# Retention's values and gate as products of halves, beside the merge gates, at the end of the attention

## The chip, the cores and the metric

The kernel runs on one core of a Trainium2 chip. The time is the device time of one launch in microseconds (us), the median of several executions. The core has five engines that run beside each other: TensorE (PE, matrix products), VectorE (DVE), ScalarE (ACT), GpSimd (POOL) and SyncE (SP, which here issues DMAs). [...]

## The reference

Two layers work on 512 tokens of width 1024, in float32. Cut to what matters:

```python
h = rmsnorm(x, norm_w) * (1 + scale) + shift
qa, ka, va, za, qr, kr, vr, zr, ga, gr = split(h @ w_in)
y_att = softmax-weighted sum of 3 groups of dilated window attention(qa, ka, va) * silu(za)
y_ret = groupnorm(retention(rotary(qr), rotary(kr), vr)) * gn_w * silu(zr)   # 4 heads of width 256
merged = sigmoid(ga) * (y_att @ w_proj_attn) + sigmoid(gr) * (y_ret @ w_proj_ret)
x = x + gate * (merged @ w_out)
```

`vr`, `zr`, `ga` and `gr` are each a product of `h` (512x1024) with 1024 columns of `w_in`.

## The kernel before, in words

**Numbers as two halves.** Each float32 operand of a product is split into a high and a low part (`split`: ACT copies the high part, DVE subtracts it, which gives the low part), and each product is three matmuls: high by high, high by low, low by high (`mm3`, L180 to L187). Weights come in tiles of 128x1024 (tag `wst`) by DMA on SP's queue and are split into `wh` and `wl`.

**Projections.** `proj_T` (L313) gives 256 columns transposed: 48 matmuls of 128x512. `proj_tok` (L331) gives 256 columns with tokens on the partitions: 96 matmuls of 128x256. `pair` (L719) gives 1024 columns by a scheme of seven products of halves in place of eight (Strassen's kind): both operands are cut in two by two, sums and differences of the parts are formed, and seven products "11", "12", "S1", "S4", "S2", "S3", "22", of 24 matmuls of 128x512 each, 168 in all, are added up to the four quarters of the result. The sums of the weights' parts are formed by DMAs that accumulate into a `wst` tile (issued by POOL); the sums of `h` are formed once by `combine_h` on POOL; those of the retention's result by `combine_y` on DVE.

**A layer in the order of the program** (`layer`, L960). Queries, keys, values and scores of the attention, for two pairs of heads; `softmax(1)` (L517: 16 exponentials on ACT, short vector work on DVE and POOL, then the probabilities are scaled in place, L563 to L569). Then, in turn, `ret_q(0)`, `attend(1, 0)`, `ret_k(0)`, `attend(1, 1)`, `ret_z(0)`. An `attend` (L573) transposes the probabilities on PE (L587), splits them (tag `pt`, four tiles), multiplies them with the values into two PSUM banks (tag `po`, a pool of two) for two rounds, and evicts with ACT (L606) and DVE (L607, L620). Then come four retention heads: `ret_q`, `ret_k` (`proj_T` and a rotation on DVE and POOL), `ret_z` (`proj_T` and a silu), `ret_scores`, `ret_v` (`proj_tok`), and for the head before `ret_out` (group norm) and `ret_y` (transposes on PE, then on DVE the norm's weight and the gate z in one step, L709). Behind them stand `combine_h`, `za`, the gates GA and GR as two `pair`s, `combine_y`, and the merges, among them `merge_ret`, a `pair` that multiplies the retention's result with its weights, and the output, a `pair` again.

**What sets the order.** [...] A scheduler lays each engine's instructions out once, near to the order of the program, and mixes neighbouring steps where one waits for another engine; tile pools (`wst` 7, `wh` and `wl` 4, `pt` 4, `qk` 6, `s` 4, `v` 6, `tmp` 4) hold a step back until a tile is free. So `attend(1, 0)` and `attend(1, 1)` stand on PE within the matmuls of the steps around them.

Of the kernel before, what the change touches and what calls it, by code (L numbers as in the profile page):

```python
# [28 lines left out]
QR, KR, VR, ZR = 5120, 6144, 7168, 8192  # L29
GA, GR = 9216, 10240  # L30
CW = 256
# [30 lines left out]
def trunk(ctx, tc, x, c, positions, norm_w, w_ada, b_ada, w_in, ret_gn_w, w_proj_attn, w_proj_ret,  # L62
          w_out, final_norm_w, c_small, c_decay, out):
    nc = tc.nc
# [9 lines left out]
    def T(tag, dt=F32, shape=(P, S)):  # L74
        n_of[tag] = n_of.get(tag, 0) + 1
        return big.tile(list(shape), dt, tag=tag, name=f"{tag}{n_of[tag]}", bufs=NB[tag])
# [5 lines left out]
    def PS(tag="mm"):  # L82
        n_of[tag] = n_of.get(tag, 0) + 1
        return psp.tile([P, S], F32, tag=tag, name=f"ps_{tag}{n_of[tag]}", bufs=NPS[tag])

    def small(shape, name, bufs=2, dt=F32):
        n_of[name] = n_of.get(name, 0) + 1
        return st.tile(list(shape), dt, tag=name, name=f"{name}{n_of[name]}", bufs=bufs)

    def f(ap):  # L90
        return ap.bitcast(F32)

    def blk(ap, b):
        return ap[:, b * P:(b + 1) * P]
# [7 lines left out]
    xs = [T("s", F32, (P, D)) for b in range(4)]  # L102
    dram = ctx.enter_context(tc.tile_pool(name="dram", bufs=1, space=bass.MemoryType.DRAM))
    x1d = dram.tile([S, D], F32, name="x1d")
    cs = const.tile([P, NSMALL], F32, name="cs")
    rows = T("tmp")[0:64, 0:P]

# [32 lines left out]
    def vec(l, what, k, n=1):  # L140
        i = {"norm": 8 * l, "gn": 16 + 8 * l, "bshift": 32 + 16 * l, "bscale": 40 + 16 * l}[what] + k
        return vecT[:, i:i + n]


    def rsqrt(src, scale, n, name):

        t = small([P, n], name + "_t", 4)
        nc.vector.tensor_scalar(t, src, scale, EPS, op0=ALU.mult, op1=ALU.add)
        r = small([P, n], name, 4)
        nc.gpsimd.tensor_tensor(r, t, mhalf[:, 0:n], op=ALU.pow)  # L150
        return r

    def split(src, hi, lo, in_order=False):

        for ins in (nc.scalar.copy(hi, src), nc.vector.tensor_tensor(lo, src, f(hi), op=ALU.subtract)):  # L155
            if in_order:
                tc.keep_in_program_order(ins)
# [22 lines left out]
    def mm3(ps_ap, pairs, first=True, last=True, skip=False):  # L180

        n, i = 3 * len(pairs), 0
        for (ah, al), (bh, bl) in pairs:
            for a, b_ in ((ah, bh), (ah, bl), (al, bh)):
                nc.tensor.matmul(ps_ap, a, b_, start=first and i == 0, stop=last and i == n - 1,  # L185
                                 skip_group_check=skip)
                i += 1  # L187
# [116 lines left out]
    class Layer:  # L304
# [345 lines left out]
        def ret_k(self, hd):  # L650
            self.rk = self.rotated(KR, hd)

        def ret_z(self, hd):
            t = T("s", F32, (P, 2, S))
            self.rz = [self.silu(ps, t[:, i]) for i, ps in enumerate(self.proj_T(ZR + hd * CW))]

        def ret_v(self, hd):
            self.rv = self.proj_tok(VR + hd * CW, blk)

        def ret_scores(self, hd):  # L660
            dec = T("dec")
# [13 lines left out]
        def ret_out(self, hd):  # L675
            self.rn = []
            for b2 in range(2):
                ps, n_ = PS("aux"), T("tmp")
                for i in range(2):
                    b = 2 * b2 + i  # L680
                    mm3(ps[:, i * CW:(i + 1) * CW],
                        [((blk(self.pts[j][0], b - j), blk(self.pts[j][1], b - j)), self.rv[j])
                         for j in range(b + 1)])
                mv = small([P, 2, 2], "mv")
                for i in range(2):
                    stats = small([P, 6], "stats", 4)
                    nc.vector.bn_stats(stats, ps[:, i * CW:(i + 1) * CW])
                    nc.vector.bn_aggr(mv[:, i], stats)
                rs = rsqrt(mv[:, :, 1], 1.0, 2, "rs")
                for i in range(2):  # L690
                    o = slice(i * CW, (i + 1) * CW)
                    nc.vector.tensor_scalar(n_[:, o], ps[:, o], mv[:, i, 0:1], rs[:, i:i + 1],
                                            op0=ALU.subtract, op1=ALU.mult)
                    self.rn.append(n_[:, o])
            self.rzs = self.rz

        def ret_y(self, hd):
            yt = T("y", F32, (P, 2, S))
            self.ytiles.append(yt)
            ys = [yt[:, 0], yt[:, 1]]  # L700
            for b2 in range(2):
                ps = PS("aux")
                for j in range(2):
                    for i in range(2):
                        nc.tensor.transpose(ps[:, (2 * i + j) * P:(2 * i + j + 1) * P],
                                            self.rn[2 * b2 + j][:, i * P:(i + 1) * P], ident)
                o = slice(b2 * CW, (b2 + 1) * CW)
                for i in range(2):
                    nc.vector.scalar_tensor_tensor(ys[i][:, o], ps[:, i * CW:(i + 1) * CW],  # L709
                                                   vec(self.l, "gn", 2 * hd + i), self.rzs[i][:, o],  # L710
                                                   op0=ALU.mult, op1=ALU.mult)
            self.y += ys


# [157 lines left out]
        def combine_h(self):  # L872
            def terms(r, c, i):
                return [f(ts[2 * c + i][:, :, r * CW:(r + 1) * CW]) for ts in self.parts]
            self.A = self.combined(terms, 4, ["qk", "qk", "s", "s", "qk", "qk", "qk", "qk"], nc.gpsimd, own=False)
            for name, k0, b0 in (("11", 0, 0), ("12", 4, 0), ("22", 4, 2)):
                self.A[name] = lambda k, u, k0=k0, b0=b0: (blk(self.hh[k0 + k], b0 + u), blk(self.hl[k0 + k], b0 + u))


        def gates(self, off, tag):  # L880

            g = [T(tag, F32, (P, 2, S)) for _ in range(4)]
            at = lambda r, c, u: g[2 * r + u][:, c]
            self.pair(self.win, 0, KT, off, self.A, at,
                      lambda r, c, u, ap: nc.scalar.activation(at(r, c, u), ap, AF.Sigmoid))
            return g

        def combine_y(self):

# [70 lines left out]
    def layer(L, xin, on_block):  # L960

        if L.l:
            L.values0(0)
            L.q(0, 0)
            L.k(0, 0)
        for pr in range(2):
            if pr:
                L.q(1, 0)
                L.attend(0, 0)
                L.k(1, 0)  # L970
                L.attend(0, 1)
            for g in (1, 2):
                L.q(pr, g)
                L.scores(pr, g - 1)
                L.k(pr, g)
            if pr:
                L.values0(1)
                L.scores(1, 2)
                L.softmax(1)
            else:  # L980
                L.values(1)
                L.scores(0, 2)
                L.softmax(0)
                L.values(2)
        L.ret_q(0)
        L.attend(1, 0)
        L.ret_k(0)
        L.attend(1, 1)
        L.ret_z(0)
        L.ret_scores(0)  # L990
        L.ret_v(0)
        for hd in range(1, RETH):
            L.ret_q(hd)
            L.ret_out(hd - 1)
            L.ret_k(hd)
            L.ret_y(hd - 1)
            L.ret_z(hd)
            L.ret_scores(hd)
            L.ret_v(hd)
        L.combine_h()  # L1000
        L.za(0)
        L.ret_out(RETH - 1)
        L.za(1)
        L.ga = L.gates(GA, "v")
        L.ret_y(RETH - 1)
        L.gr = L.gates(GR, "pt")
        L.combine_y()
        L.merge_ret()
        L.merge_att()
        L.combine_m()  # L1010
        L.result(xin, on_block)
# [13 lines left out]
    def next_layer(b, x_, r):  # L1025
# [5 lines left out]
        if b == 3:  # L1031
            L1[0].transposed(xn[0:2], 0, 4, KT)
            L1[0].transposed(xn[2:4], 2, 0, KT)

    layer(L0, x, next_layer)
    for m in range(4):
        background.append(gate_row(1, m))
    fw = []

    def result(b, xt, r):  # L1040
# [4 lines left out]
        for i in range(2):  # L1045
# [6 lines left out]
            nc.sync.dma_start(out[b * P:(b + 1) * P, i * S:(i + 1) * S], o)  # L1052

    layer(L1[0], x1d, result)


# [21 lines left out]
```

## Time and profile before

| | us |
|---|---|
| median of 3 runs | 1374.93 (1373.93 to 1375.13) |
| profiled execution | 1373.44 |
| its span | 1371.6 |
| PE busy | 1321.6 (96%) |
| DVE busy | 950.7 (69%) |
| ACT busy | 582.7 (42%) |
| POOL busy | 292.3 (21%) |
| DMA queue of hardware, of software, share of 16 engines | 33.5%, 14.5% |
| mean granted clock of TensorE | 0.994 of full speed |

The span runs from the first instruction to the last; 1.84 us of the profiled execution lie outside of it. PE is busy nearly always, so a stretch's length is the sum of PE's work in it, and time is won where PE has less to do and lost where PE waits. In a row of a timeline, the start of the next row, less the start of this one, is what an instruction really takes, since matmuls are pipelined and overlap in the records.

### The profile page before, as it was taken

Reading aid. Unit: us, or ns where it says so; the run is one execution under the profiler, and the core shown is the slowest. Engines: PE = TensorE matmul, PEld = TensorE weight load, DVE = VectorE, ACT = ScalarE, POOL = GpSimd, SP = SyncE. Lnnn points to the kernel's source line nnn. Section 1 sums busy time; section 2 is a strip of 40 time slices with the busy share of each in tenths; the row PEclk is TensorE's granted clock in tenths of the full one; section 3 lists DMA queues with packets and bytes.
Section 4 is the critical chain, followed back from the end, with each engine's and each line's share of the span. In section 5 each row is a group of like instructions: output and inputs, shape, how many; then the busy total and the mean of one; then the engine's idle time right before and its main releaser. Section 6 shows DMA issues by size and latency. Waiting matters only on the chain.

```text
span 1371.6 us, 18119 instructions
## 1 busy us (share of the span) xinstructions
PE 1321.6 (96%) x6857; PEld 1144.2 (83%) x6857; DVE 950.7 (69%) x1592; ACT 582.7 (42%) x991; POOL 292.3 (21%) x288
## 2 busy tenths in 40 slices
PE   4999999999999999999989999999999999999996
PEld 4779988989889887888768899888989889778875
DVE  5997669586564577766888646656765566868678
ACT  5442433263223245763643325334422323566355
POOL 1200200041121383220230002002121027622124
PEclk9999999999999999999999999999999999999998
DMA  9954245332232228994974323232223232688673
GB/s 315 316 187 128 87 129 184 93 93 70 70 93 86 77 62 184 200 198 140 199 230 154 101 92 92 62 92 77 62 86 100 70 93 68 118 193 201 173 160 101
DMA packets 136647, 179.54 MB, mean 131 GB/s; under 512 B 5936, under 2 KB 97264, under 8 KB 136560
## 3 DMA queue, kind: packets, MB, share of 16 engines
q1 hardware_dynamic: 119152, 144.83, 33.5%
q0 software_dynamic: 17408, 33.56, 14.5%
q8 instruction: 54, 0.88, 0.3%
q14 instruction: 33, 0.27, 0.1%
HBM read 174.17 MB, written 4.19 MB: 130 GB/s over the span
## 4 chain that ended last, share of the span: by engine, by line
PE 79%; DVE 9%; DMA 4%; issue 3%; POOL 2%; ACT 2%; POOLq 0%; SPq 0%; ACTq 0%; DVEq 0%
PE ps_mm L185 67%; PE ps_aux L185 5%; DMA wst<-in_w_in 3%; DVE wl L155 3%; PE ps_po L185 2%; PE ps_po L191 1%; DVE qk L155 1%; PE ps_aux L587 1%; POOL tmp L852 1%; PE ps_aux L191 1%; ACT wh L155 1%; PE ps_po L192 1%; DMA pt<-in_x 1%; PE ps_aux L930 0%; DVE tmp L952 0%
## 5 line engine op out<-in xcount | busy, mean ns | idle before, releaser
L185 PE MATMUL ps_mm<-h,wh 128*128 128x512 f32 x1664 | 524.1, 394 | 5.8 <-POOL h L302 2.1
L155 DVE TENSOR_TENSOR wl<-wst,wh 128x1024 fp32r<-128x1024 f32 (+1 forms) x266 | 344.5, 1300 | 173.4 <-ACT wh L155 167.8
L155 ACT CAST wh<-wst 128x1024 fp32r<-128x1024 f32 (+1 forms) x266 | 277.0, 1045 | 336.1 <-PE ps_mm L185 249.2
L185 PEld LDWEIGHTS ps_mm<-h,wh 128*128 128x128 f32 x1664 | 310.2, 189 | 69.2 <-POOL h L302 2.7
L185 PE MATMUL ps_mm<-h,wl 128*128 128x512 f32 x832 | 325.7, 392 | 0.0
L185 PE MATMUL ps_mm<-wh,h 128*128 128x256 f32 (+1 forms) x1248 | 309.8, 335 | 10.7 <-POOL h L302 2.2
L185 PEld LDWEIGHTS ps_mm<-wh,h 128*128 128x128 f32 x1248 | 236.1, 216 | 27.8 <-ACT h L155 3.3
L185 PE MATMUL ps_mm<-wl,h 128*128 128x256 f32 (+1 forms) x624 | 207.0, 333 | 0.0
L185 PEld LDWEIGHTS ps_mm<-h,wl 128*128 128x128 f32 x832 | 156.8, 189 | 31.8
L185 PEld LDWEIGHTS ps_mm<-wl,h 128*128 128x128 f32 x624 | 134.7, 216 | 5.6
L641 POOL TENSOR_TENSOR tmp<-tmp,tmp 128x512 f32<-128x512 f32 x32 | 50.8, 1598 | 353.2 <-ACT wh L155 259.5
L185 PE MATMUL ps_mm<-wh,qk 128*128 128x512 f32 x384 | 122.4, 394 | 2.6 <-DVE s L806 2.3
L185 PEld LDWEIGHTS ps_mm<-wh,qk 128*128 128x128 f32 x384 | 72.8, 190 | 19.5 <-DVE s L806 2.7
L185 PE MATMUL ps_mm<-wl,qk 128*128 128x512 f32 x192 | 74.5, 393 | 0.0
L185 PE MATMUL ps_mm<-wh,s 128*128 128x512 f32 x224 | 72.1, 391 | 0.0
L155 ACT CAST qk<-ps_mm 128x512 fp32r<-128x512 f32 x48 | 27.7, 584 | 91.2 <-PE ps_mm L185 91.2
L155 ACT CAST qk<-tmp 128x512 fp32r<-128x512 f32 x60 | 36.4, 620 | 69.8 <-POOL tmp L641 49.7
L155 DVE TENSOR_TENSOR v<-ps_mm,v 128x256 fp32r<-128x256 f32 (+1 forms) x52 | 23.9, 460 | 53.9 <-ACT v L155 53.8
L213 DVE SCALAR_TENSOR_TENSOR tmp<-pt,sc,tmp 128x256 f32<-128x256 f32 x126 | 58.1, 494 | 0.3
L155 DVE TENSOR_TENSOR qk<-tmp,qk 128x512 fp32r<-128x512 f32 x60 | 46.9, 798 | 12.6 <-ACT qk L155 12.3
L736 POOL DMA_DIRECT2D wst<-in_w_in x32 | 39.0, 1232 | 76.3 <-DVE wl L155 68.8
L541 POOL COPY mlc<-ml 32x4 f32<-32x4 f32 x32 | 7.1, 221 | 200.3 <-ACT s L532 198.9
(226 smaller groups left out, 1728.0 us busy)
## 6 DMA issues: line engine op xcount, KB each, us to landing
wst<-in_w_in SPq DMA_DIRECT2D x162, 512.0 KB, 3.6
pt<-in_w_ada SPq DMA_DIRECT2D x36, 512.0 KB, 5.1
wst<-in_w_in POOLq DMA_DIRECT2D x32, 512.0 KB, 7.4
wst<-in_w_proj_ret POOLq DMA_DIRECT2D x16, 512.0 KB, 6.1
wst<-in_w_out POOLq DMA_DIRECT2D x16, 512.0 KB, 5.9
wst<-in_w_proj_ret SPq DMA_DIRECT2D x12, 512.0 KB, 5.3
wst<-in_w_out SPq DMA_DIRECT2D x12, 512.0 KB, 4.1
wst<-in_w_proj_attn SPq DMA_DIRECT2D x8, 512.0 KB, 4.4
```

Of the source, the lines that this page charges most:

```text
L155: for ins in (nc.scalar.copy(hi, src), nc.vector.tensor_tensor(lo, src, f(hi), op=ALU.subtract)):
L185: nc.tensor.matmul(ps_ap, a, b_, start=first and i == 0, stop=last and i == n - 1, skip_group_check=skip)
L191: nc.tensor.matmul(ps_ap, st[0], mv, start=first, stop=False, skip_group_check=skip)
L192: nc.tensor.matmul(ps_ap[:, 0:P], st[1], mv[:, 0], start=False, stop=last, skip_group_check=skip)
L213: nc.vector.scalar_tensor_tensor(acc, w_, c_, acc, op0=ALU.mult, op1=ALU.add)
L541: (nc.gpsimd if cc % 2 else nc.vector).tensor_copy(mlc[32 * b:32 * b + 32, cc], ml0[32 * cc:32 * cc + 32, b])
L587: nc.tensor.transpose(blk(ps, j), src, ident)
L641: nc.gpsimd.tensor_tensor(a, a, b_, op=ALU.subtract if i == 0 else ALU.add)
L736: nc.gpsimd.dma_start(t, part(r, c, i), accum_op=ALU.add)
L852: eng.tensor_tensor(t, t, a, op=ALU.subtract)
```

## The change

`vr` and `zr` are now computed by `pair`, for all four heads at once, and so are GA and GR; the four pairs stand in a row behind the attention (`keep`), and their results go, through tiles of tag `v`, to four arrays in DRAM (`kept`). The retention loads a head's raw values and its silu(z) from there (`ret_vz`) and splits the values; the merge loads the gates (`kept_rows`). `combine_h` moves ahead of the four pairs. The multiplication by silu(z) moves into `ret_out`, one DVE instruction a tile, and `ret_y` evicts on ACT with the norm's weight as its scale. `ret_q(0)` and `ret_k(0)`, which stood between the attends, stand behind the four pairs.

```diff
-        def ret_z(self, hd):
-            t = T("s", F32, (P, 2, S))
-            self.rz = [self.silu(ps, t[:, i]) for i, ps in enumerate(self.proj_T(ZR + hd * CW))]
-
-        def ret_v(self, hd):
-            self.rv = self.proj_tok(VR + hd * CW, blk)
+        def ret_vz(self, hd):
+            raw, self.rz = T("s", F32, (P, 4, CW)), T("s", F32, (P, 4, CW))
+            for o, what in ((raw, "vr"), (self.rz, "zr")):
+                nc.sync.dma_start(o, kept[self.l, what][:, hd * CW:(hd + 1) * CW].rearrange("(b p) j -> p b j", p=P))
+            self.rv = []
+            for i2 in range(2):
+                t = T("v", F32R, (P, 2, 2, CW))
+                split(raw[:, 2 * i2:2 * i2 + 2], t[:, :, 0], t[:, :, 1])
+                self.rv += [(t[:, j, 0], t[:, j, 1]) for j in range(2)]
...
-            self.rzs = self.rz
+                nc.vector.tensor_tensor(n_, n_, self.rz[:, 2 * b2:2 * b2 + 2].rearrange("p b j -> p (b j)"), op=ALU.mult)
...
-                    nc.vector.scalar_tensor_tensor(ys[i][:, o], ps[:, i * CW:(i + 1) * CW],
-                                                   vec(self.l, "gn", 2 * hd + i), self.rzs[i][:, o],
-                                                   op0=ALU.mult, op1=ALU.mult)
+                    nc.scalar.activation(ys[i][:, o], ps[:, i * CW:(i + 1) * CW], AF.Copy,
+                                         scale=vec(self.l, "gn", 2 * hd + i))
...
-            self.A = self.combined(terms, 4, ["qk", "qk", "s", "s", "qk", "qk", "qk", "qk"], nc.gpsimd, own=False)
+            self.A = self.combined(terms, 4, ["qk"] * 6 + ["s"] * 2, nc.gpsimd, own=False)
...
+        def keep(self, off, what, act):
+
+            def done(r, c, u, ap):
+                o = T("v")
+                act(o, ap)
+                nc.sync.dma_start(kept[self.l, what][(2 * r + u) * P:(2 * r + u + 1) * P, c * S:(c + 1) * S], o)
+            self.pair(self.win, 0, KT, off, self.A, lambda r, c, u: T("pt"), done)
+
+        def kept_rows(self, what, tag):
+            res = []
+            for b in range(4):
+                t = T(tag, F32, (P, 2, S))
+                nc.sync.dma_start(t, kept[self.l, what][b * P:(b + 1) * P].rearrange("p (c j) -> p c j", c=2))
+                res.append(t)
+            return res
...
-        L.ret_q(0)
         L.attend(1, 0)
-        L.ret_k(0)
         L.attend(1, 1)
-        L.ret_z(0)
+        L.combine_h()
+        L.keep(VR, "vr", nc.scalar.copy)
+        L.keep(ZR, "zr", lambda o, ap: L.silu(ap, o))
+        L.keep(GA, "ga", L.sigmoid)
+        L.keep(GR, "gr", L.sigmoid)
+        L.ret_q(0)
+        L.ret_k(0)
+        L.ret_vz(0)
         L.ret_scores(0)
-        L.ret_v(0)
         for hd in range(1, RETH):
...
-        L.combine_h()
         L.za(0)
         L.ret_out(RETH - 1)
         L.za(1)
-        L.ga = L.gates(GA, "v")
+        L.ga = L.kept_rows("ga", "v")
         L.ret_y(RETH - 1)
-        L.gr = L.gates(GR, "pt")
+        L.gr = L.kept_rows("gr", "pt")
         L.combine_y()
```

The order moves at three places. PE before, at the start of `attend(1, 0)` of the first layer (`ps_mm49` and `ps_mm50` are products of `ret_z(0)`, `ps_aux62` and `ps_aux63` take the attend's first transposes):

```order
L185 MATMUL ps_mm49_2838<-h4_99,wl44_2835 128x512
L185 MATMUL ps_mm50_2863<-h1_96,wh43_2828 128x512
L587 MATMUL ps_aux62_2600<-cs_76,s11_2153 128x128 x4
L587 MATMUL ps_aux63_2608<-cs_76,s12_2398 128x128 x4
L185 MATMUL ps_mm50_2863<-h5_100,wh43_2828 128x512
L185 MATMUL ps_mm50_2863<-h1_96,wl43_2829 128x512
L185 MATMUL ps_mm50_2863<-h1_96,wh43_2828 128x512
L185 MATMUL ps_mm50_2863<-h5_100,wh43_2828 128x512
```

PE of the changed kernel, the same place (`ps_mm48` is the product "S1" of `vr`, with `qk31` and `qk32` from `combine_h`; `ps_po11` and `ps_po12` are the attend's products with the values):

```order
L186 MATMUL ps_mm48_2840<-wl44_2790,qk31_2677 128x512
L186 MATMUL ps_mm48_2840<-wh44_2789,qk32_2678 128x512
L588 MATMUL ps_aux62_2530<-cs_84,s11_2161 128x128 x4
L588 MATMUL ps_aux63_2538<-cs_84,s12_2406 128x128 x4
L588 MATMUL ps_aux64_2546<-cs_84,s9_1946 128x128 x4
L192 MATMUL ps_po11_2562<-pt37_2535,v9_1199 128x256
L193 MATMUL ps_po11_2562<-pt37_2535,v9_1199 128x128
L192 MATMUL ps_po12_2563<-pt37_2535,y5_1255 128x256
L193 MATMUL ps_po12_2563<-pt37_2535,y5_1255 128x128
L588 MATMUL ps_aux65_2554<-cs_84,s9_1946 128x128 x3
```

Of `vr`'s pair two products stand ahead of the attend: the 24 matmuls of "11" in the middle of the last `scores(1, 2)`, the 24 of "S1" behind it. From the first transpose on, nothing but the two attends stands on PE until the last of them. PE before, within the attends (`ps_mm52` is `ret_v(0)`):

```order
L191 MATMUL ps_po14_2655<-pt40_2628,v14_2342 128x256
L192 MATMUL ps_po14_2655<-pt40_2628,v14_2342 128x128
L185 MATMUL ps_mm52_2982<-wh45_2944,h2_97 128x256
L185 MATMUL ps_mm52_2982<-wl45_2945,h2_97 128x256
L185 MATMUL ps_mm52_2982<-wh45_2944,h6_101 128x256
L185 MATMUL ps_mm52_2982<-wh46_2950,h3_98 128x256
L185 MATMUL ps_mm52_2982<-wl46_2951,h3_98 128x256
L587 MATMUL ps_aux68_2768<-cs_76,s10_1959 128x128 x4
L185 MATMUL ps_mm52_2982<-wh46_2950,h7_102 128x256
L587 MATMUL ps_aux69_2776<-cs_76,s10_1959 128x128 x3
```

PE of the changed kernel, at the attends' end (`ps_po19` is the product "12" of `vr`):

```order
L192 MATMUL ps_po18_2658<-pt44_2632,v13_2295 128x256
L193 MATMUL ps_po18_2658<-pt44_2632,v13_2295 128x128
L192 MATMUL ps_po18_2658<-pt43_2625,v14_2350 128x256
L193 MATMUL ps_po18_2658<-pt43_2625,v14_2350 128x128
L192 MATMUL ps_po18_2658<-pt44_2632,v14_2350 128x256
L193 MATMUL ps_po18_2658<-pt44_2632,v14_2350 128x128
L186 MATMUL ps_po19_2793<-wh41_2747,h3_106 128x512
L186 MATMUL ps_po19_2793<-wl41_2748,h3_106 128x512
```

The "12" of `vr` takes a `po` bank as the attends do, and stands behind them all; no matmul of another step is left between. DVE before, `combine_y` among the splits of GA's weights (`wl84` to `wl88`, `v28`, `s20` and `tmp99` are `combine_y`):

```order
L155 TENSOR_TENSOR wl84_4869<-wst76_4733,wh84_4868 128x1024
L155 TENSOR_TENSOR v28_5296<-y13_4220,v27_5295 128x512
L155 TENSOR_TENSOR v28_5296<-y14_5000,v27_5295 128x512
L155 TENSOR_TENSOR s20_5290<-y11_3280,s19_5289 128x512
L155 TENSOR_TENSOR s20_5290<-y12_3750,s19_5289 128x512
L838 TENSOR_TENSOR tmp99_5310<-y12_3750,y14_5000 128x512
L155 TENSOR_TENSOR wl85_4899<-wst79_4822,wh85_4898 128x1024
```

DVE of the changed kernel, `combine_y` (`tmp98`, `tmp99`, `v60`, `h10`, `qk54`) among the splits of `merge_ret`'s own weights (`wl121` to `wl123`):

```order
L842 TENSOR_TENSOR tmp98_5253<-y11_4339,y13_4925 128x512
L156 TENSOR_TENSOR wl121_5386<-wst87_5381,wh121_5385 128x1024
L156 TENSOR_TENSOR v60_5240<-y14_5210,v59_5239 128x512
L842 TENSOR_TENSOR tmp99_5254<-y12_4632,y14_5210 128x512
L156 TENSOR_TENSOR h10_5246<-tmp98_5253,h9_5245 128x512
L156 TENSOR_TENSOR s28_5568<-y10_2561,s27_5567 128x1024
L856 TENSOR_TENSOR tmp98_5253<-tmp98_5253,y11_4339 128x512
L156 TENSOR_TENSOR h10_5246<-tmp99_5254,h9_5245 128x512
L156 TENSOR_TENSOR wl122_5390<-wst88_5382,wh122_5389 128x1024
```

Of the 22 DVE instructions of `combine_y`, 19 now stand among those of `merge_ret`; the gates' 168 and 168 matmuls, under which they stood, are gone from there.

## Rows read from the trace of the kernel before

**Rows 1.** The page's part 1: each engine's busy time and share.
```profile
PE 1321.6 (96%) x6857; PEld 1144.2 (83%) x6857; DVE 950.7 (69%) x1592; ACT 582.7 (42%) x991; POOL 292.3 (21%) x288
```

**Rows 2.** A window of layer 1: length; PE, PEld, DVE, ACT, POOL busy; clock; DMA.
```profile
940.26:960.50 20.24, 20.24 (x91) 16.71 (x91) 16.63 (x42) 11.43 (x39) 10.23 (x15) 1.00 0.25 79
```

**Rows 3.** Timeline of PE, ret_v's and ret_z's matmuls: start, length, engine, line, tiles.
```profile
322.13 0.40 PE L185 MATMUL ps_mm<-wh,h 128*128 128x256 f32 x2
...
322.49 0.40 PE L185 MATMUL ps_mm<-wh,h 128*128 128x256 f32 x2
...
327.20 0.62 PE L185 MATMUL ps_mm<-h,wh 128*128 128x512 f32 x2
...
327.88 0.39 PE L185 MATMUL ps_mm<-h,wh 128*128 128x512 f32 x1
```

**Rows 4.** Timeline of PE in layer 1: last scores, what follows, first transposes.
```profile
940.20 0.22 PE L192 MATMUL ps_aux<-qk,qk 128*128 128x128 f32 x1
940.26 0.45 PE L185 MATMUL ps_mm<-h,wl 128*128 128x512 f32 x1
...
960.51 1.03 PE L587 MATMUL ps_aux<-cs,s 128*128 128x128 f32 x8
961.30 0.48 PE L185 MATMUL ps_mm<-h,wh 128*128 128x512 f32 x1
```

**Rows 5.** Timeline of DVE, softmax of layer 1.
```profile
942.30 1.23 DVE L155 TENSOR_TENSOR wl<-wst,wh 128x1024 fp32r<-128x1024 f32 x1
...
951.83 0.68 DVE L155 TENSOR_TENSOR qk<-tmp,qk 128x512 fp32r<-128x512 f32 x1
...
953.28 1.23 DVE L155 TENSOR_TENSOR wl<-wst,wh 128x1024 fp32r<-128x1024 f32 x1
...
955.89 1.29 DVE L563 TENSOR_TENSOR s<-s,f 128x512 f32<-128x512 f32 x2
```

**Rows 6.** The window of the attends, ps_po's instructions alone.
```profile
294.40:318.80 24.40, 7.32 (x60) 7.24 (x60) 5.43 (x9) 2.38 (x4) 1.00 0.21 66
```

**Rows 7.** Groups of DVE by form, 294.4 to 318.8, the attends of layer 0.
```profile
L155 DVE TENSOR_TENSOR pt<-ps_aux,pt 128x512 fp32r<-128x512 f32 x6 | 3.9, 682 | 0.3 <-ACT pt L155 0.2
L620 DVE TENSOR_TENSOR y<-ps_po,y 128x256 f32<-128x256 f32 x5 | 3.0, 620 | 0.4 <-PE ps_po L192 0.4
L607 DVE TENSOR_TENSOR y<-ps_po,y 128x256 f32<-128x256 f32 x4 | 2.4, 629 | 0.8 <-ACT y L606 0.8
...
L155 DVE TENSOR_TENSOR pt<-ps_aux,pt 128x384 fp32r<-128x384 f32 x2 | 1.1, 543 | 0.0
```

**Rows 8.** Groups of ACT by form, 274 to 318.8.
```profile
L155 ACT CAST pt<-ps_aux 128x512 fp32r<-128x512 f32 x6 | 3.3, 589 | 3.6 <-PE ps_aux L587 3.6
...
L606 ACT COPY y<-ps_po 128x256 f32<-128x256 f32 x4 | 2.4, 654 | 0.6 <-PE ps_po L192 0.6
```

**Rows 9.** Timeline of PE: two places behind idle time, in brackets.
```profile
16.83 1.02 PE L225 MATMUL ps_aux<-one,tmp 128*128 128x1 f32 x4 [10.40 <-DVE tmp L213]
...
25.83 0.63 PE L185 MATMUL ps_mm<-h,wl 128*128 128x512 f32 x1
...
690.79 0.50 PE L185 MATMUL ps_mm<-wh,qk 128*128 128x512 f32 x1 [2.26 <-DVE s L806]
```

**Rows 10.** Windows: behind that second wait; one retention head.
```profile
691.90:695.40 3.50, 3.50 (x10) 2.71 (x9) 3.39 (x11) 1.45 (x4) 0.00 (x0) 0.51 0.99 308
...
1043.70:1096.20 52.50, 52.50 (x304) 46.54 (x304) 30.00 (x53) 15.21 (x22) 7.47 (x6) 1.00 0.29 86
```

**Rows 11.** Groups of DVE by form in that head.
```profile
L155 DVE TENSOR_TENSOR wl<-wst,wh 128x1024 fp32r<-128x1024 f32 x9 | 11.8, 1308 | 13.0 <-ACT wh L155 12.9
```

**Rows 12.** Windows: merge_ret, then GA, of layer 0.
```profile
591.26:623.90 32.64, 32.64 (x146) 27.03 (x144) 23.67 (x25) 17.18 (x20) 7.24 (x6) 1.00 0.92 205
508.63:550.37 41.74, 40.71 (x179) 32.53 (x180) 32.40 (x40) 24.76 (x34) 16.49 (x13) 1.00 0.70 154
```

**Rows 13.** The page's part 6: a weight tile's load, from issue to landing.
```profile
wst<-in_w_in SPq DMA_DIRECT2D x162, 512.0 KB, 3.6
```

More of the change, by code (lines that the diff above doesn't have):

```diff
@@ L104, in trunk @@
     x1d = dram.tile([S, D], F32, name="x1d")
+    kept = {(l, what): dram.tile([S, D], F32, name=f"{what}{l}") for l in range(DEPTH) for what in ("vr", "zr", "ga", "gr")}
     cs = const.tile([P, NSMALL], F32, name="cs")
@@ L874, in terms, with sigmoid @@
                 return [f(ts[2 * c + i][:, :, r * CW:(r + 1) * CW]) for ts in self.parts]
-            self.A = self.combined(terms, 4, ["qk", "qk", "s", "s", "qk", "qk", "qk", "qk"], nc.gpsimd, own=False)
+            self.A = self.combined(terms, 4, ["qk"] * 6 + ["s"] * 2, nc.gpsimd, own=False)
             for name, k0, b0 in (("11", 0, 0), ("12", 4, 0), ("22", 4, 2)):
                 self.A[name] = lambda k, u, k0=k0, b0=b0: (blk(self.hh[k0 + k], b0 + u), blk(self.hl[k0 + k], b0 + u))
[L880 to L886, printed above, removed]
+        def keep(self, off, what, act):
[4 more added lines that the diff above has]
+            self.pair(self.win, 0, KT, off, self.A, lambda r, c, u: T("pt"), done)
+        def sigmoid(self, o, ap):
+            nc.scalar.activation(o, ap, AF.Sigmoid)
+        def kept_rows(self, what, tag):
[5 more added lines that the diff above has]
+            return res
         def combine_y(self):
@@ L984, in layer @@
                 L.values(2)
+        L.attend(1, 0)
+        L.attend(1, 1)
+        L.combine_h()
[3 more added lines that the diff above has]
+        L.keep(GR, "gr", L.sigmoid)
         L.ret_q(0)
-        L.attend(1, 0)
         L.ret_k(0)
-        L.attend(1, 1)
-        L.ret_z(0)
+        L.ret_vz(0)
         L.ret_scores(0)
-        L.ret_v(0)
         for hd in range(1, RETH):
@@ L996, in layer @@
             L.ret_y(hd - 1)
-            L.ret_z(hd)
+            L.ret_vz(hd)
             L.ret_scores(hd)
-            L.ret_v(hd)
-        L.combine_h()
         L.za(0)
```

## The prediction

> **What bounds the kernel now.** I read the busy times first: PE 1321.6 of 1371.6 us, no other engine over 70% [rows 1]. Then the windows by stage: behind the attention's last scores PE is busy for all 20.24 us up to the attends [rows 2], and the retention's windows are the same (one is shown below); no wait is left there that a change could take away. So a stage gets shorter only by fewer or narrower matmuls, and longer by whatever leaves PE without work. The change does both, and I cost the two sides apart. In a row of the timeline the reader is to look at the distance between starts, not at the length.
>
> **What it removes on PE.** The step of a group of three matmuls (high by high, high by low, low by high) is 0.36 us for 128x256, from 322.13 to 322.49, and 0.68 us for 128x512, from 327.20 to 327.88 [rows 3]: 0.120 and 0.227 each. Per layer `ret_v` has 4 x 96 of the first, 46.1 us, and `ret_z` 4 x 48 of the second, 43.5 us; the two pairs that replace them have 2 x 168 of the second, 76.2 us. That saves 13.4 us a layer, 26.9 in both. GA and GR are pairs before and after and cost PE the same.
>
> **What it uncovers: the softmax.** Before the change, `ret_q(0)`, `ret_k(0)` and a part of `ret_z(0)` lie between the last scores and the first transposes, from 940.26 to 960.51 [rows 4]. In the changed order that place holds "S1" of `vr`, 24 matmuls or 5.4 us. The chain under it is scores, maxima, exponentials, denominators, factors, and the scaling of the probabilities: its first two instructions on DVE begin at 955.89 and take about 0.65 each [rows 5], so what the first transposes need is there at 956.6, 16.3 us behind the last scores. 16.3 less 5.4 leaves PE idle for 10.9 us a layer. The low end: the two weight splits of 1.23 and two qk splits of some 0.6 that stand within the chain [rows 5] belong to other steps and could fall out of it, 3.7 us, which leaves 7.2. The high end: as many other splits get in as two more of 1.3, so 13.5. `combine_h`'s work for POOL stands there too, but between softmax's short copies, so I take the middle value, which is what this chain has taken.
>
> **What it uncovers: the attends.** Before, both attends are spread over 24.4 us of PE work, of which their products take 7.32 [rows 6]; eight transposes step in 0.79 [rows 4], so their 30 take 3.0. Now they stand alone. PE needs 10.3 us for them. DVE needs for each three splits of 0.68, one of 0.54, two additions of 0.63 and four of 0.62 [rows 7]: 6.3, for both 12.6, with two splits of `combine_h` of 0.68 between them 13.9. In addition, each step waits for the one before: four transposes (0.4), the copy on ACT (0.59) [rows 8], the split (0.68), the products, then the eviction (0.65 and 0.63) [rows 7, 8] before a bank of the pool of two is free, and for a second attend once more. Walking through the printed order with these durations I come to 18.3 us, an estimate, which is near the middle between the bounds 13.9 (DVE without a gap) and 24.4 (as long as before). The wait is 18.3 less 10.3, 8.0 a layer, from 3.6 to 14.1.
>
> **The clock.** [...] Behind the longer wait of 10.40 us at the start, matmuls of 128x512 still take 0.63 us in place of 0.39, 9.0 us later [rows 3, 9]: a loss of 4.5. [...] I take 3.2.
>
> [...]
>
> **The retention.** A head has 52.50 us of PE and 30.00 of DVE [rows 10]. Without V and Z, PE has 52.5 less 11.5 less 10.9, 30.1. DVE loses the splits of V's and Z's four weight tiles, 4 x 1.31 [rows 11], and is at 24.8; the splits of the loaded values, the multiplication with z and the moved eviction change it by less than 1 us. That is 82% in place of 57%, and there is less foreign work to hide `ret_out`'s norm, the new multiplication and the transposes of `ret_y`, one after the other. I take 1.5 us of waits a layer (0 to 4).
>
> **The merge.** `combine_y` was hidden under GA and GR, 168 matmuls each. Now 19 of its 22 DVE instructions stand in `merge_ret`. That stage has DVE 23.67 of 32.64 us for 146 matmuls [rows 12], so 27.6 for all 168 (38.1 us); 19 instructions of 128x512 at 0.68 [rows 7] add 12.9: 40.5. DVE is then later than PE by 2.4, and as the products ask for the parts in an order, I take 3.0 a layer (0, if much of it is done under `za`, to 5).
>
> **What I cost at nothing.** The four pairs in a row: GA alone lost 41.74 less 40.71, 1.0 us [rows 12], and the weights' splits (1.3 us, two for 24 matmuls or 5.4 us) fit. The results to DRAM are 16 stores a pair's column on SP's queue, of 2 MB for 38 us of PE; a weight tile lands 3.6 us after its issue [rows 13], and `wst` holds seven. The loads back are needed long after the stores, and `ret_vz(0)` comes behind GA and GR, 76 us later. If this cover fails, it is rival D.
>
> **The sum.** 2 x (10.9 + 8.0 + 3.2 + 1.5 + 3.0) = 53.2, less 26.9, gives +26.3. On the profiled execution's 1373.44 that is 1399.7; the median lies 1.5 above it, so 1401. With all low ends 2 x 12.5 less 26.9, 1371.5; with all high ends (13.5, 14.1, 4.5, 4, 5) 2 x 41.1 less 26.9, 1428.7.
>
> **The rivals.**
> B, not slower: the waits take their low ends. The saving of 13.4 us a layer is certain, so the kernel is no slower if softmax and attends together leave PE idle for less than that: 7.2 + 3.6 + 1.7, 12.5, gives 1373 on the median. For it: the chain before was not hurried, since nothing waited for it, and DVE's foreign work in it is half other. Against it: both low ends are needed at once, and the exponentials on ACT and the steps of the attend follow from data.
> C, DVE and its chain bound the retention: the load of z, the norm, the multiplication, the transposes and the eviction leave PE waiting in every head. At 3 us for each of 8 heads in place of my 3.0 in all, +21: 1422. For it, DVE at 82%; against it, ACT at 15.21 of 52.5 [rows 10], which takes the eviction over.
> D, weights come late: a pair's second weight tile stands behind the stores on SP's queue and misses its time by one landing, 3.6 us [rows 13], in the three later pairs of each layer: +21.6, 1423. For it, one queue for both; against it, seven tiles and the mean traffic.
> [...]
>
> **How the numbers follow.** My forecast 0.63, B 0.14, C 0.09, D 0.07, E 0.07. The forecast's own range is 1386 to 1414: each of the two large terms can be off by some 3 us a layer. To leave out no more than 2 in 10, the range takes in E and half of C and D, and the upper half of B: 1375 to 1422. A measurement of this kernel can tell some 0.2%, 2.75 us, from no change. B is half below 1372.2, half within; a little of the forecast's low edge is added: faster 0.08, same 0.07, slower 0.85.
>
> **What would show it.** The saving: retention heads of about 30 us, V's and Z's pairs of 38 each. The softmax: a wait of PE of about 11 us behind "S1", put down to DVE's scaling, in each layer. The attends: a stretch of some 18 us, PE busy for little more than half of it, with waits on DVE's splits and evictions. The clock: a granted clock near 0.5 there, and for some us of the product "12". `merge_ret`: waits on DVE's splits of its weights or of `combine_y`. I am wrong if PE's idle time from the last scores to the product "12" is under 13 us a layer, if waits in the retention or in the four pairs are as large as those in the attends, or if PE's busy time falls by something else than 27 us and the clock's loss.

## The result and the profile after

The changed kernel takes 1435.28 us (median of 4 runs, 1434.16 to 1440.25) against 1374.72 us, a ratio of 1.0459 (95% interval 1.0439 to 1.0479). It is slower by some 60 us; 26 were forecast. The profiled execution took 1435.49 us, 62.05 more than that of before.

First the page's part 1 and two lines of its part 2, 40 slices of the span, in tenths:

```profile
PE 1318.2 (92%) x6377; PEld 1119.1 (78%) x6377; DVE 1013.4 (71%) x1608; ACT 640.6 (45%) x1071; POOL 330.0 (23%) x320
...
PE   4899999859999999989989999994899999998996
...
PEclk9999999979999999999999999997999999999998
```

PE is busy for only 3.4 us less than before [rows 1], though it has 26.9 us less to do at full speed: by that, matmuls at a lower granted clock (a mean of 0.972 over the span) took some 23.5 us back (an estimate; a part of them stands where PE waits for others anyway). Idle time grew by 65.5 us, and the 9th and the 28th slice of 40, one in each layer, show a dip in PE and in the clock. The groups of PE's waits name them (engine, line and what it waited for; us in total, times, longest):

```profile
PE ps_aux L588 <- DVE s L564: 27.5, 2, 14.6
...
PE ps_mm L186 <- ACT h L156: 9.2, 6, 3.4
PE ps_mm L186 <- DVE pt L810: 8.5, 6, 2.1
PE ps_aux L588 <- DVE pt L156: 6.8, 6, 2.2
...
PE ps_mm L186 <- ACT h L783: 4.3, 2, 2.1
...
PE ps_aux L710 <- DVE tmp L700: 3.0, 2, 1.5
```

The first is the transposes' wait for the scaled probabilities, once in each layer; L810 and L783 are the pairs' results, L156 with `pt` the attends' splits, L156 with `h` the sums' splits (3.4 us of it in each `merge_ret`), L700 the multiplication by z of the last head.

PE's timeline in layer 1, which answers to [rows 4]: the last scores end at 968.47, "S1" runs from there, and the first transposes begin 21.2 us later, 14.62 of them idle.

```profile
968.41 0.22 PE L193 MATMUL ps_aux<-qk,qk 128*128 128x128 f32 x1
968.47 0.68 PE L186 MATMUL ps_mm<-wh,qk 128*128 128x512 f32 x2
969.75 0.50 PE L186 MATMUL ps_mm<-wl,qk 128*128 128x512 f32 x1 [0.60 <-DVE wl L156]
...
974.64 0.39 PE L186 MATMUL ps_mm<-wh,qk 128*128 128x512 f32 x1
989.65 1.73 PE L588 MATMUL ps_aux<-cs,s 128*128 128x128 f32 x7 [14.62 <-DVE s L564]
```

What DVE did in that time (against [rows 5]), and POOL beside it:

```profile
969.61 0.74 DVE L508 TENSOR_TENSOR s<-ps_aux,cs 128x256 f32<-128x256 f32 x2
970.28 1.64 DVE L156 TENSOR_TENSOR wl<-wst,wh 128x1024 fp32r<-128x1024 f32 x1
...
972.51 1.12 DVE L156 TENSOR_TENSOR qk<-tmp,qk 128x512 fp32r<-128x512 f32 x1
...
974.14 3.16 DVE L156 TENSOR_TENSOR qk<-tmp,qk 128x512 fp32r<-128x512 f32 x1
977.22 1.22 DVE L525 TENSOR_TENSOR m<-mx,mx 128x8 f32<-128x8 f32 x1
978.36 1.21 DVE L156 TENSOR_TENSOR wl<-wst,wh 128x1024 fp32r<-128x1024 f32 x1
979.50 0.16 DVE L528 TENSOR_SCALAR nm<-m 128x8 f32<-128x8 f32 x1
...
988.79 1.31 DVE L564 TENSOR_TENSOR s<-s,f 128x512 f32<-128x512 f32 x2
```

```profile
967.32 5.75 POOL L860 TENSOR_TENSOR tmp<-tmp,h 128x512 f32<-128x512 f32 x3 [0.63 <-DVE qk L156]
...
974.52 2.22 POOL L847 TENSOR_TENSOR tmp<-h 128x512 f32<-128x512 f32 x1
976.82 1.60 POOL L848 TENSOR_TENSOR tmp<-tmp,tmp 128x512 f32<-128x512 f32 x1
...
987.42 2.12 POOL L559 COPY f<-f0c 32x2 f32<-32x2 f32 x8 [4.72 <-DVE f L556]
```

The maxima (`nm`) are ready 11.0 us behind the last scores (968.47 to 979.50); before the change it was 3.4 (940.26 to 943.64):

```profile
943.64 0.17 DVE L527 TENSOR_SCALAR nm<-m 128x8 f32<-128x8 f32 x1
```

The splits of the weights (`wl`) and of `combine_h`'s sums (`qk`) stand ahead of them, and one split of 0.68 us [rows 5] takes 3.16 while POOL adds. From the maxima to the scaling it is 9.3 us. In layer 0 the whole takes 23.2 us.

Windows (columns as in [rows 2]): both attends of layer 0 and of layer 1; a stretch of 32.5 us of the retention; the last 120 matmuls of `merge_ret`.

```profile
297.69:317.68 19.99, 14.84 (x91) 13.60 (x91) 15.21 (x24) 8.80 (x17) 4.96 (x5) 0.76 0.01 2
989.65:1009.80 20.15, 14.84 (x90) 13.45 (x91) 15.35 (x25) 9.27 (x18) 4.95 (x5) 0.75 0.00 1
```

```profile
508.20:540.70 32.50, 32.50 (x169) 27.85 (x168) 23.88 (x42) 11.60 (x19) 8.44 (x6) 1.00 0.30 90
```

```profile
618.53:653.68 35.15, 29.58 (x121) 23.61 (x121) 33.92 (x42) 19.56 (x28) 8.26 (x7) 0.95 0.71 152
```

The attends alone take 20 us at a mean granted clock of 0.76. The retention has no gap; its stretch holds 168 matmuls where a head has 158, so that ten (2.3 us) are of a neighbouring step, and a head takes 30.2 us, as forecast. And `merge_ret`'s 120 matmuls (27.2 us at full speed) take 35.15, with DVE busy for 33.92 of them, where 146 took 32.64 and DVE 23.67 before [rows 12].

The bill by stages, start to start on PE, per layer (layer 0, layer 1), against before:

| stage | lost, us |
|---|---|
| fewer and wider matmuls | -13.4, -13.4 |
| last scores to first transposes, less 5.4 of "S1" | 17.8, 15.7 |
| the attends, less 10.3 of PE's work | 9.7, 9.8 |
| the four pairs, over 168 x 0.227 each, less what GA and GR lost before | 4.2, 8.5 |
| the retention's loop | 0, 0 |
| `merge_ret` (46.1 in place of 38.1) and the last `ret_y` | 9.9, 9.9 |
| elsewhere | 1.8, 1.8 |

The sum is 30.0 and 32.3 us, 62.3 together, against the 62.1 us by which the span grew.

### The profile page after: what moved, and what is told of

Read it like the earlier page. It is cut to its first block, busy times and chain, and to the rows that moved or that the text cites. A ratio compares the mean times of both kernels' runs of the same rounds, so it can differ in the third digit from the quotient of the medians.

```text
span 1433.7 us, 17686 instructions
## 1 busy us (share of the span) xinstructions
PE 1318.2 (92%) x6377; PEld 1119.1 (78%) x6377; DVE 1013.4 (71%) x1608; ACT 640.6 (45%) x1071; POOL 330.0 (23%) x320
## 5 line engine op out<-in xcount | busy, mean ns | idle before, releaser
L156 DVE TENSOR_TENSOR wl<-wst,wh 128x1024 fp32r<-128x1024 f32 (+1 forms) x290 | 374.2, 1295 | 208.8 <-ACT wh L156 199.1
L186 PE MATMUL ps_mm<-h,wh 128*128 128x512 f32 x1408 | 447.7, 395 | 5.8 <-POOL h L303 2.1
L156 ACT CAST wh<-wst 128x1024 fp32r<-128x1024 f32 (+1 forms) x290 | 302.2, 1045 | 298.5 <-PE ps_mm L186 171.7
L186 PEld LDWEIGHTS ps_mm<-h,wh 128*128 128x128 f32 x1408 | 263.5, 189 | 60.1 <-POOL h L303 2.7
L186 PE MATMUL ps_mm<-wh,h 128*128 128x512 f32 (+1 forms) x864 | 258.9, 379 | 22.4 <-ACT h L156 9.2
L186 PE MATMUL ps_mm<-h,wl 128*128 128x512 f32 x704 | 276.1, 393 | 0.0
L186 PEld LDWEIGHTS ps_mm<-wh,h 128*128 128x128 f32 x864 | 182.1, 229 | 46.5 <-ACT h L156 11.8
L186 PE MATMUL ps_mm<-wh,qk 128*128 128x512 f32 x576 | 180.8, 392 | 8.2 <-ACT h L783 4.3
L186 PE MATMUL ps_mm<-wl,h 128*128 128x512 f32 (+1 forms) x432 | 162.0, 376 | 0.0
L186 PEld LDWEIGHTS ps_mm<-wh,qk 128*128 128x128 f32 x576 | 108.8, 189 | 32.5 <-ACT h L783 5.1
L156 ACT CAST qk<-tmp 128x512 fp32r<-128x512 f32 x60 | 36.9, 620 | 87.9 <-POOL tmp L642 64.9
L156 ACT CAST qk<-ps_mm 128x512 fp32r<-128x512 f32 x48 | 27.7, 584 | 90.3 <-PE ps_mm L186 90.3
L186 PE MATMUL ps_po<-wh,h 128*128 128x512 f32 (+1 forms) x224 | 66.3, 369 | 0.2 <-DVE y L621 0.2
L186 PEld LDWEIGHTS ps_mm<-wl,qk 128*128 128x128 f32 x288 | 54.3, 189 | 15.5 <-DVE wl L156 4.2
L156 DVE TENSOR_TENSOR qk<-tmp,qk 128x512 fp32r<-128x512 f32 x60 | 56.4, 941 | 12.7 <-ACT qk L156 11.9
L186 PEld LDWEIGHTS ps_mm<-wh,s 128*128 128x128 f32 x288 | 54.1, 188 | 13.9 <-ACT pt L804 2.9
```

## The experiments

Each ran beside the kernel before on the same chip, and ratios to that are compared (the changed kernel's is 1.0459). Lines are those of the changed kernel.

**e1: no sums.** The edit:

```diff
-            self.A = self.combined(terms, 4, ["qk"] * 6 + ["s"] * 2, nc.gpsimd, own=False)
-            for name, k0, b0 in (("11", 0, 0), ("12", 4, 0), ("22", 4, 2)):
+            self.A = {}
+            for name, k0, b0 in (("11", 0, 0), ("12", 4, 0), ("22", 4, 2), ("S1", 0, 2), ("S4", 4, 2), ("S2", 0, 2), ("S3", 0, 0)):
```

> The sums of h's halves (combine_h: GpSimd additions, ScalarE and VectorE splits) are left out; the products take unsummed parts of h in their place, as many matmuls as before. Theory A (combine_h's work gets into the softmax's chain, on VectorE's queue and by slowing VectorE while GpSimd adds): from the last scores to the first transposes it takes about 15 us in place of 21.2 to 23.2, and the kernel about 1421 us (2 x 7 less than 1435). Rival (the chain is longer because of the pair's weight splits and because ScalarE starts late): the chain stays above 19 us, the kernel above 1429 us.

Measured: 1419.22 us, ratio 1.0328 (1.0304 to 1.0352). PE from its last product to the transposes, and DVE's maxima:

```profile
278.33 0.39 PE L186 MATMUL ps_mm<-wh,h 128*128 128x512 f32 x1
288.09 1.94 PE L588 MATMUL ps_aux<-cs,s 128*128 128x128 f32 x8 [9.38 <-DVE s L564]
```

```profile
276.52 0.17 DVE L525 TENSOR_TENSOR m<-mx,mx 128x8 f32<-128x8 f32 x1
276.72 0.17 DVE L528 TENSOR_SCALAR nm<-m 128x8 f32<-128x8 f32 x1
...
287.25 1.29 DVE L564 TENSOR_TENSOR s<-s,f 128x512 f32<-128x512 f32 x2
```

The last scores end at 273.02, so the chain takes 15.1 us and not 23.2, and the maxima are there after 3.7. Theory A holds: `combine_h`'s work is what lengthened the chain. Of the 7.3 us by which the maxima are later in the changed kernel (layer 1), some 4.4 are longer instructions there: splits of 3.16 and 1.12 us in place of 0.68, one of 1.64 in place of 1.21, and L525 of 1.22 in place of 0.17 (an estimate from the rows); the rest is more instructions ahead of the maxima, `combine_h`'s two splits among them. `merge_ret` stays at 46.1 in layer 0 (48.3 in layer 1).

**e2: the sums late.** `combine_h`'s results go to `["s"] * 4 + ["y"] * 4` in place of `["qk"] * 6 + ["s"] * 2`.

> combine_h's results go to tiles that the attention still holds (4 of s, 4 of y), so its splits cannot start before the attends; S1 then stands among the attends' matmuls and not ahead of them. Theory A: the chain shrinks to about 15 us, its 5.4 us of cover by S1 is lost but comes back as cover in the attends: about 1422 us. Rival A2 (GpSimd's additions alone, which need only tmp tiles, slow VectorE): the chain stays at 19 us or more, all of it idle, and the kernel is at 1432 us or above. Rival (weight splits): as A2, but VectorE's splits have their usual length of 0.7 and 1.2 us in the chain.

Measured: 1424.22 us, ratio 1.0364 (1.0339 to 1.0390). The chain takes 13.8 us, 13.60 of them idle, and GpSimd does none of its additions there, since they wait behind the splits.

```profile
274.27 0.22 PE L193 MATMUL ps_aux<-qk,qk 128*128 128x128 f32 x1
288.09 1.30 PE L588 MATMUL ps_aux<-cs,s 128*128 128x128 f32 x5 [13.60 <-DVE s L564]
```

Theory A again; A2 was not tested by it, as the additions moved too.

**e3: cover at the attends.** e2's tiles and

```diff
+        L.ret_q(0)
         L.attend(1, 0)
+        L.ret_k(0)
         L.attend(1, 1)
...
-        L.ret_q(0)
-        L.ret_k(0)
         L.ret_vz(0)
```

> ret_q(0) and ret_k(0) stand between the attends again, with combine_h's results in s and y tiles as in e2; everything else as in the changed kernel. Theory (the loss at softmax and attends is missing cover): 14.6 us of ret_q(0) and ret_k(0) and 5.4 us of the product 11 cover a chain of 15 to 16 us, and the attends have 24 + 18 matmuls as cover; per layer some 15 + 5 us of waits and 3 us of slow clock go: about 1390 us. Rival (VectorE is the limit there, the wait only moves into the attends and the pairs): less than 20 us gained, above 1415 us.

Measured: 1405.29 us, ratio 1.0224 (1.0208 to 1.0241), between the two. The wait for the softmax is gone (the transposes follow the product "11" at once), but a wait of 8.2 us stands within the attends, for splits of `pt`.

**e5 and e6: the sums on VectorE.** In the changed kernel (e5) and in e3 (e6): `nc.vector` in place of `nc.gpsimd` in `combine_h`.

> The changed kernel with one edit: combine_h adds on VectorE in place of GpSimd. Theory A2 (what stretches VectorE's splits in the softmax's chain, 3.16 us for one of 0.68, is GpSimd adding from SBUF beside it): splits in the chain have 0.7 and 1.2 us again; VectorE has 6 additions of 0.68 of its own there (4 us), so the chain shrinks from 21.2 to 23.2 to about 18 to 19 us: some 1428 us. Rival (VectorE is simply overloaded there): 22 additions of 0.68 more on it make the chain and the attends longer, 1436 us or above.

> The kernel of e3 with combine_h's additions on VectorE. In e3 two weight splits took 4.26 us together and others 3.5 to 3.9 beside GpSimd's additions, and the attends waited 8.2 + 1.5 + 2.2 us. Theory A2: these waits fall to some 5 us a layer in all: about 1391 us (1405 less 2 x 7). Rival (VectorE has too much work in the attends, whoever slows it): 1403 us or above.

Measured: e5 1436.12 us, ratio 1.0459 (1.0437 to 1.0480), no gain; e6 1395.85 us, ratio 1.0170 (1.0139 to 1.0202), by the ratios some 7 us better than e3. In e5 every split in the chain has its usual length again (0.68 and 1.21), and the chain takes 20.3 us, but VectorE's own additions stand in it, and the attends take 22.6 us in place of 20.0. So the stretching goes where GpSimd's additions go, but the load on VectorE decides there, in whichever form it comes. In e6 GpSimd still has the scaling and the rotation to do, and two weight splits of 1.23 us took 4.26 together beside it. The same two took 4.26 in e3, and the wait for the splits of `pt` stays (8.3 us in e6, 8.2 in e3): `combine_h`'s additions on GpSimd did not cause that wait, and where e6 gains was not traced.

```profile
284.83 1.23 DVE L156 TENSOR_TENSOR wl<-wst,wh 128x1024 fp32r<-128x1024 f32 x1
...
292.27 4.26 DVE L156 TENSOR_TENSOR wl<-wst,wh 128x1024 fp32r<-128x1024 f32 x2
```

```profile
291.76 1.49 POOL L570 TENSOR_TENSOR s<-s,f 128x512 f32<-128x512 f32 x1
293.21 4.45 POOL L642 TENSOR_TENSOR tmp<-tmp,tmp 128x512 f32<-128x512 f32 x2
```

**e4 and e7 to e12: cover for `combine_y`.** GA and GR go back to their place ahead of the merges, which needs a second `combine_h` there, since its eight tiles cannot be kept through the retention:

```diff
-        L.keep(GA, "ga", L.sigmoid)
-        L.keep(GR, "gr", L.sigmoid)
...
+        L.combine_h(["qk", "qk", "s", "s", "qk", "qk", "qk", "qk"])
         L.za(0)
         L.ret_out(RETH - 1)
         L.za(1)
-        L.ga = L.kept_rows("ga", "v")
+        L.ga = L.gates(GA, "v")
         L.ret_y(RETH - 1)
-        L.gr = L.kept_rows("gr", "pt")
+        L.gr = L.gates(GR, "pt")
```

> GA and GR are computed at their old place ahead of the merges, with a second combine_h there; V and Z as in the changed kernel. Theory B (merge_ret lost the cover of combine_y, 9.9 us a layer): merge_ret is back at 38 to 39 us, and 2 x 9 us come back: about 1417 us. Rival (merge_ret waits for weights, since 3 loads and 4 accumulations stand close together): merge_ret stays above 44 us, the kernel above 1430 us. Rival (the second combine_h slows VectorE in the last heads): merge_ret recovers, but heads get longer by 3 us or more: about 1424 us.

e4 took 1462.47 us, ratio 1.0645 (1.0626 to 1.0664). `merge_ret` is back at 38.1 us in both layers, but GA waits once for 23.5 us in each:

```profile
PE ps_mm L186 <- DVE tmp L626: 46.9, 2, 23.5
```

GA's matmuls need the PSUM banks of za, which its silu (L625 on ACT, L626 on DVE) frees; the silu needs `tmp` tiles, and the second `combine_h` holds them through 38 us of additions on GpSimd, from 520 to 558 us in layer 0; the silu begins at 557. Six kernels tried to get that work out of the way: e7 (za ahead of it, and `v` in place of `s` tiles), e8 (as e7, with e6's start and za(0) between the attends), e9 (e6 with the second `combine_h` on VectorE, ahead of za), e10 (as e9, za(0) between the attends), e11 (as e10, the second `combine_h` behind ret_out(3) and za(1)), e12 (as e10, 6 `tmp` and 6 `wst` tiles).

> As e4 (GA and GR at their old place, a second combine_h on GpSimd), but za's two multiplications stand ahead of the second combine_h on GpSimd and its results need no s tile, which e4 waited for. Theory B (combine_y lost its cover): no wait of 23 us; merge_ret at 38 to 39 us; about 1436 - 2 x 9 = 1418 us. Rival (merge_ret waits for its weights): merge_ret stays above 44 us. Rival (GA and GR beside combine_h and combine_y lose as much as merge_ret gains): 1430 us or above, with waits of 5 us and more in GA.

> V and Z as pairs, with cover for all three places: ret_q(0), ret_k(0) and za(0) between the attends, combine_h's additions on VectorE with results in s and y tiles, GA and GR ahead of the merges as in the kernel before. Theory (the loss was only missing cover): of the saved 26.9 us the waits take back some 3 us at the attends and 3 in the pairs per layer: about 1374 - 27 + 12 = 1359 us, faster than the kernel before. Rival (two combine_h and the round trip take it back): 1372 us or above.

> The kernel of e6 (cover at the attends, combine_h on VectorE) with GA and GR back at their old place and a second combine_h on VectorE ahead of za, which covers it with 21.8 us. In e8 the second combine_h on GpSimd came late (36 us of additions that began 14 us after the last scores) and cost some 34 us a layer. Theory B (merge_ret lost combine_y's cover, nothing else): merge_ret at 38.1 us, GA waits under 3 us a layer; 1396 less 2 x 8 is about 1380 us. Rival (VectorE is full at that place, so the wait only moves from merge_ret to GA): 1392 us or above.

> As e9, with za(0) between the attends as in e8, so that only za(1) and GA's first two products cover the second combine_h. From e8: 1434 less 2 x 34 us of waits at the second combine_h gives 1366 us; some 2 us a layer may be left at GA: about 1370 us, the same as the kernel before or a little faster. Rival (VectorE is full at GA): waits of 5 us a layer or more there, 1380 us or above.

> As e10, with the second combine_h behind ret_out(3) and za(1) in the program, so that it no longer stands ahead of ret_out's normalization in VectorE's queue and takes tmp tiles later. e10 lost 19.0 us a layer in one wait of ret_y(3) there. Theory (the wait in e10 is queue order and tmp tiles, not VectorE's load): that wait goes; the second combine_h's first sums come 4 to 8 us late for GA: 1412 - 2 x 13 = 1386 us. Rival (VectorE's load): the same 19 us appear in GA, 1408 us or above.

> As e10, with 6 tmp tiles in place of 4 and 6 wst tiles in place of 7. If e10's wait of 19.0 us is for a tmp tile that combine_h holds, it goes, and the kernel is at about 1375 us. If VectorE's order is the cause, the wait stays above 12 us and the kernel at 1395 us or above; if 6 weight tiles are too few, waits for weights show in the pairs and the heads.

| kernel | us | ratio | its new wait, each layer |
|---|---|---|---|
| e7 | 1471.59 | 1.0710 (1.0690 to 1.0730) | 11.9 and 11.9 in GA |
| e8 | 1434.15 | 1.0439 (1.0418 to 1.0460) | 7.6 and 12.9 to 14.5 in GA |
| e9 | 1410.28 | 1.0276 (1.0245 to 1.0308) | 12.8 in GA |
| e10 | 1411.97 | 1.0284 (1.0259 to 1.0309) | 19.0 ahead of ret_y(3) |
| e11 | 1401.75 | 1.0202 (1.0168 to 1.0237) | about 6 ahead of ret_y(3), 4 to 6 in GA |
| e12 | 1414.41 | 1.0300 (1.0265 to 1.0335) | 19.7 in GA |

Theory B holds for `merge_ret` in all: with GA and GR ahead of it, it takes 38.1 us (39.0 in one layer of e8), whatever else was changed; with `combine_y` uncovered, 44.3 to 48.9 (the changed kernel, e1 to e3, e5, e6). Its window in e10 is that of before to a hundredth [rows 12]:

```profile
610.48:643.12 32.64, 32.64 (x146) 27.03 (x144) 23.66 (x25) 17.20 (x20) 7.25 (x6) 1.00 0.92 205
```

The forecasts of e4 and e7 to e12 were all too low, and the waits point to one reason: the second `combine_h` had no room. Before the change it began on GpSimd 36 us ahead of GA (at 472 and 509 us in layer 0), under `ret_v(3)` and za; now a head is 22 us shorter, and it begins when GA needs it. In e10 VectorE is busy but for 0.7 us through the wait, with the sums ahead of the normalization in its queue; e12's two more `tmp` tiles only moved the wait to L626. e11 puts the sums behind the normalization: some 10 to 12 us of the 19 stay, so that neither theory of its forecast holds alone. That points to the queue's order and load, not to the tile; it was not taken further.

No version here beats the kernel before. The nearest is e6, though e11's interval overlaps with its.

## Why the prediction was right and wrong

The direction, the saving and the place of the losses were right; the size was not, +62 in place of +26. The saving is borne out by the stages: 30.2 us a head in the changed retention, no gap, and pairs of 38.1 us where nothing waits (GR).

**The softmax was mis-sized: 10.9 us a layer in the sum, 17.8 and 15.7 measured.** The step took the old chain of 16.3 us over and held that `combine_h`'s work would stand "between softmax's short copies". In this stretch it does not: GpSimd adds from 967.32 to 978.42, and its copies begin at 987.42. The work also put splits on VectorE ahead of the maxima, and the splits beside GpSimd's additions are stretched. e1 and e2, which take just that out, bring the chain to 15.1 and 13.8. The trace before had such a stretched split to read, beside `combine_h` at its old place, where nothing waited for it:

```profile
497.51 5.14 DVE L155 TENSOR_TENSOR wl<-wst,wh 128x1024 fp32r<-128x1024 f32 x1
```

```profile
498.70 2.85 POOL L856 TENSOR_TENSOR tmp<-tmp,h 128x512 f32<-128x512 f32 x2
```

Beside GpSimd's work one split of 0.68 us took 3.16 in the changed kernel, and two of 1.23 took 4.26 in e3 and in e6; e5 (ratio 1.0459, as the changed kernel) shows that avoiding it gains nothing when VectorE must do the additions instead.

**The merge was mis-sized: 3.0 in the sum, 9.9 measured.** The step found DVE the later engine (40.5 us against 38.1), and DVE was nearly full there (33.92 of 35.15), but it took the excess for the wait. `combine_y` and the products are a chain: the last head's multiplication, transposes and evictions come first (a wait of 1.5 there), "S1" waits for its sum's split (3.4), "S2" for the copy of the first product, late on ACT (2.1), and the clock falls behind the waits (0.95 in the stretch). The stretching counts here too: ahead of the sum for "S1" stands a weight split of 3.49 us in place of 1.21, while GpSimd multiplies for za, in both layers.

```profile
618.38 3.49 DVE L156 TENSOR_TENSOR wl<-wst,wh 128x1024 fp32r<-128x1024 f32 x1
621.79 0.68 DVE L842 TENSOR_TENSOR tmp<-y,y 128x512 f32<-128x512 f32 x1
```

```profile
617.82 2.96 POOL L632 TENSOR_TENSOR y<-y,tmp 128x512 f32<-128x512 f32 x2
```

```profile
623.18 0.57 PE L186 MATMUL ps_mm<-wh,h 128*128 128x512 f32 x1 [3.43 <-ACT h L156]
```

`merge_ret` takes 46.1 us. Its cause, the lost cover, is shown by the kernels with GA and GR at their old place.

**The attends**: 8.0 in the sum, 9.7 and 9.8 measured. The walk of 18.3 us was 1.7 short, but it had no slow clock in it, which was a term of its own, 3.2. That was the author's estimate, and no run shows it. Its low end, 1.7, is half of the 3.50 us at a clock of 0.51 [rows 10]; its high end, 4.5, is half of the 9.0 us behind the wait at the start, of which PE was busy for 7.00, and there the profile has matmuls of 0.63 us but gives the clock as 1.00. What the runs showed in its place: behind the softmax's wait (12.88 and 14.62 us of idle time) the granted clock was 0.50 for the first 8.3 us of the attends (9.3 in layer 1), and 1.00 for the next 10.3:

```profile
297.69:306.00 8.31, 6.10 (x28) 5.70 (x29) 5.94 (x8) 3.36 (x7) 4.96 (x5) 0.50 0.00 1
306.00:316.30 10.30, 7.36 (x57) 6.52 (x57) 8.21 (x15) 5.25 (x10) 0.00 (x0) 1.00 0.01 2
```

PE was busy for 6.1 us at 0.50, half of which, 3.1, is the clock's cost (an estimate), close to that term. How much of it lengthened the attends, whose steps also wait for each other, was not separated.

**The pairs were put at nothing: 4.2 and 8.5 measured.** The reason given was that GA alone had lost 1.0 us. In the row of four, PE waits for L810 three times in each layer, 0.7 to 2.1 us each. Behind two of these waits, 1.5 us in layer 0 and 2.1 in layer 1, the next 48 matmuls ran at different clocks:

```profile
342.90:354.00 11.10, 11.10 (x49) 9.20 (x50) 5.41 (x5) 7.28 (x10) 2.42 (x2) 1.00 0.94 225
1035.90:1048.50 12.60, 12.53 (x48) 10.23 (x49) 5.87 (x7) 7.73 (x10) 2.41 (x2) 0.86 0.97 223
```

Layer 1 lost some 1.6 us so, and about as much behind a wait of 1.8 (0.85 over 11.6 us). With 0.96 and 0.90 over the rest of `vr` behind the attends, the clock makes some 1.0 us of layer 0's loss and 4.8 of layer 1's, and the waits 3.9 and 5.5, less what GA and GR lost before (estimates).

**The retention**: 1.5 in the sum, 0 measured: DVE at 23.88 of 32.5 us left room.

Of the rivals, C (VectorE bounds the retention) and D (weights late) did not come: no wait there is put down to either. E, which has 0.07 among the chances, is a clock near half through both attends: the author's estimate, which no row of before shows. It came in part, with 0.50 for 8.3 and 9.3 of the 20 us. B was far off. The range ended at 1422 and missed: the high ends set for softmax and merge, 13.5 and 5, were both passed, and the pairs had no term in it. The high ends counted durations of before, and left out what moved work does in the queues of the chain.

## What to carry to other kernels

When work is moved in front of a chain, cost the chain again with the moved work in each engine's queue, splits and additions included; a saving on the bound engine is worth only what still covers the chains behind it. Before moving a stage, list what it hides: here GA and GR hid `combine_y`, and V and Z hid the sums that GA and GR need. Here VectorE, busy for 71% of the span, held up a chain by the order of its queue (11.0 us to the maxima in place of 3.4), and where it was busy for 97% of a stage, the loss exceeded its excess of work (8.0 us in `merge_ret` in place of 2.4). Read what the moved instructions take in the trace before, beside the engines that they will run beside again.

## What the runs showed of the hardware

A split of 0.68 us on VectorE took 3.16 (the changed kernel), and two of 1.23 took 4.26 (e3, e6), beside GpSimd's work; with the additions taken from GpSimd, the splits of the softmax's chain had their usual lengths, 0.68 and 1.21 (e5). A split of 1.23 took 5.14 beside GpSimd's additions in the kernel before. GpSimd's additions stretched as well: 2.2 us each in e6 beside VectorE's splits, against a mean of 1.6 before. In the row of pairs the clock stayed at 1.00 behind a wait of 1.5 us and was 0.86 over the 12.6 us behind one of 2.1. The mean granted clock was 0.75 and 0.76 over the 20 us of the attends, with waits of 0.2 to 2.2 us each: 0.50 for 8.3 and 9.3 us behind the softmax's wait of 12.88 and 14.62, then 1.00 for 10.3, then 0.50 up to their end.
